# A ring of 21 weight tiles instead of 18, two of the tiles in a place of their own, and GpSimd's DMA scratch cut to 256 bytes

## The chip, the cores and the metric

The kernel runs on one core of one Trainium2 chip. The metric is the time of one execution on the device, in microseconds (us). Before the change the median of 3 runs is 1808.93 us, from 1807.16 to 1809.41.

The engines are named as the profile names them: PE is TensorE's matmuls, PEld its weight loads, DVE VectorE, ACT ScalarE, POOL GpSimd, SP SyncE, which only issues DMAs. A "q" behind a name (SPq) is that engine's sequencer, which issues DMAs and waits for semaphores.

## The reference

The program is a small transformer for 256 tokens of 1024 values in float32. The first block has two layers, each of a mixer (dilated attention in one half, gated linear attention in the other) and a dense SwiGLU network. The second block has one layer: modulation by a condition, a mixer of two kinds of attention, a router, and 32 experts, of which each token takes four.

```python
def second_block(x, c, w_ada, ...):
    mod = silu(c) @ w_ada + b_ada                  # 6 x 1024
    h = rms_norm(x, g_pre_mix) * (1 + sc_m) + sh_m
    proj = h @ w_in
    y_a = fox_attention(...)                       # forget gates: b_forget
    y_b = moba_attention(..., rel_bias)            # bias by distance
    x = x + gt_m * rms_norm(mix @ w_out, g_post_mix)
    h = rms_norm(x, g_pre_ffn) * (1 + sc_f) + sh_f
    x = x + gt_f * rms_norm(moe_ffn(h, ...), g_post_ffn)

def expert_block(xb, e):                           # rows of the tokens that chose e
    hdn = xb @ w_gate_up[e] + b_gate_up[e]         # 1024 -> 2048
    return clamped_swiglu(hdn) @ w_down[e] + b_down[e]   # 1024 -> 1024
```

The bias of the second attention depends on the distance of two tokens alone, so 384 values for each of 8 heads give the whole of it. The kernel writes them to DRAM once as a table (`toep`, each of the 8 rows repeated 128 times, 1536 KB), from which block 2 reads.

## The kernel before

**Weights.** All weights are read once, in tiles of 128 partitions x 2048 values, 1 MB each. SP issues the loads, in the order in which the program's scheduler puts them; a load whose place is still in use waits in SP's queue, and all loads behind it wait too. In block 1 the tiles go through the pool `ring` (4 places, `wtile()`); each is split into a high and a low part by ACT (the cast, L250) and DVE (the difference, L251), and PE multiplies three times (L256 to L258).

**Experts.** An expert is 12 tiles: 8 of `w_gate_up`, 4 of `w_down`. PE multiplies them unsplit: `g1` (L1209) takes the 8 gate_up tiles, 8 matmuls each, `act` makes the gated values `a` (tag "g"), and `g2` transposes them into `aT` (L1247) and multiplies the 4 down tiles (L1253). Experts with more than 64 tokens take a second pass under a branch (L1476, L1513). The tiles stand in the places of the ring RING2, in turn: -1 is one of the 4 places of `ring`, 0 to 7 are places of the pool `ring2`, which is opened when the second mixer's pool is closed, 8 to 12 of `ring3`, opened in the experts' phase, and HOME is the place of the hidden state, free once that is copied to DRAM (`homed`). The load of a tile waits until the matmuls of the tile 18 before it are through. The first EARLY = 10 tiles of expert 0 are asked for before the router (`first.load(EARLY)`), the rest when the pools are open.

**Block 1, first layer.** `early` work for block 2 is done there: GpSimd's queue loads `rel_bias` and `oh`, PE makes `rv` (8 x 384) from them, and GpSimd's queue stores `toep` (L821). `rv` has the tag "gkT", so that DVE's later copy gkT (L592) into the same place waits for the end of the store. The load of `bf` (L916), 8 values of the forget gate for block 2, has a place of its own that is free all along; the scheduler has it issued early, beside `gf` and `modb`, between two tiles of the first layer's `w_in`.

[...]

Of the kernel before, what the change touches and what calls it, by code (L numbers as in the profile page):

```python
# [9 lines left out]
F32 = mybir.dt.float32  # L10
# [10 lines left out]
P = 128  # L21
T = 256
D = 1024
KC = D // P
DFF = 2816
NF = DFF // P
NE = 32
# [5 lines left out]

HOME = 99
RING2 = (-1, 0, 1, -1, 2, 3, 4, 5, 6, 7, -1, -1, 8, 9, 10, 11, 12, HOME)
EARLY = 10

# [60 lines left out]
def kernel_body(ctx, tc, I, out, stop=None, dbg=None):  # L98
    nc = tc.nc
# [3 lines left out]
    xpool = ctx.enter_context(tc.tile_pool(name="xpool", bufs=1))  # L103
    spool = ctx.enter_context(tc.tile_pool(name="spool", bufs=4))
    ring = ctx.enter_context(tc.tile_pool(name="ring", bufs=4))
    dense = ctx.enter_context(ExitStack())
# [5 lines left out]
    def nm(s):  # L112
        uid[0] += 1
        return f"{s}_{uid[0]}"
# [4 lines left out]
    def wtile():  # L119
        return ring.tile([P, 2048], F32, tag="w", name=nm("w"))  # L120
# [666 lines left out]
    with ExitStack() as cx:  # L787
# [8 lines left out]
        starts = []  # L796
# [11 lines left out]
        def early():  # L808
            r = wtile()
            nc.scalar.dma_start(r[:, :9 * P], I["lev"])  # L810
            S.copy(wlev, r[:, :9 * P])
            rb = mix.tile([P, 8], F32, tag="kx", name="rb", bufs=2)
            G.memset(rb, 1.0)
            nc.gpsimd.dma_start(rb[0:NE, :], I["rel_bias"])
            oh = mix.tile([P, 384], F32, tag="X", name="oh")
            nc.gpsimd.dma_start(oh, I["oh"])
            q = ps()
            TE.matmul(q[0:8, :384], lhsT=rb, rhs=oh, start=True, stop=True)
            rv = mix.tile([8, 384], F32, tag="gkT", name="rv")
            V.tensor_copy(rv, q[0:8, :384])  # L820
            nc.gpsimd.dma_start(toep.rearrange("p a m -> a p m"), rv.unsqueeze(1).to_broadcast([8, P, 384]))  # L821
            S.activation(cond, cond, AF.Silu)
# [58 lines left out]
        def mixer2(x, start, late, done):  # L881
# [33 lines left out]
            bf = small(1, "bf", bufs=1)  # L915
            nc.sync.dma_start(bf[0:8], I["b_forget"].rearrange("o h -> h o"))  # L916
            S.activation(fT, f[0:8], AF.Identity, bias=bf[0:8, 0:1])
# [86 lines left out]
        g = {}  # L1004
# [134 lines left out]

        mixb = cx.enter_context(tc.tile_pool(name="mixb", bufs=1))  # L1140
        with tc.tile_pool(name="mix", bufs=1, side="right", reuse_waits="tile") as mix:
            rear = mixer2(x, starts[4], late_mix, done)
        ring2 = ctx.enter_context(tc.tile_pool(name="ring2", bufs=1, side="right", reuse_waits="tile"))
        turn = [0]

        def etile():
            i = RING2[turn[0] % len(RING2)]
            turn[0] += 1
            if i < 0:
                return wtile()  # L1150
            if i == HOME:
                return cpool.tile([P, 2048], F32, tag="h", name=nm("w2"))
            return (ring2 if i < 8 else ring3).tile([P, 2048], F32, tag=f"w{i}", name=nm("w2"))
# [24 lines left out]
        def expert(e):  # L1178
            return Expert(lambda kc: I["w_gate_up"][e, kc * P:(kc + 1) * P, :], lambda b: I["w_down_2"][e, b * 256:(b + 1) * 256, :], e == NE - 1)

        first = expert(0)
        first.load(EARLY)
        rear()
# [4 lines left out]
    with ExitStack() as cx:  # L1188
# [5 lines left out]
        bb = mo.tile([P, 2, 512], F32R, name="bb", bufs=1)  # L1194
        now = mo.tile([P, 9, NE], F32, name="now", bufs=1)
        qe = mo.tile([P, 2, NE], F32, name="qe", bufs=1)
# [43 lines left out]
        def g2(a, wd, y, j):  # L1240
# [3 lines left out]
            for i in range(4):  # L1244
                TE.transpose(q[:, i * P:(i + 1) * P], av[:, i // 2, i % 2, :], ident)
            aT = mo2.tile([P, 4, P], F32, tag="aT", name=nm("aT"), bufs=1)
            S.copy(aT.rearrange("p a b -> p (a b)"), q)  # L1247
# [60 lines left out]
        def extra_xt(slot0, pm):  # L1308
            op = mo.tile([P, 2, 32], F32R, tag="opos", name=nm("opos"), bufs=1)
            for t in range(2):  # L1310
                onehot(op[:, t, :], slot0, pm(t))
            xt = mo2.tile([P, KC, 32], F32, tag="aT", name=nm("oxt"), bufs=1)
            q = ps()
# [32 lines left out]
        def extra_out(a, slot0, pm, gt, wd, pg=None):  # L1346
# [7 lines left out]
            for j in range(2):  # L1354
                TE.transpose(q[:, j * P:(j + 1) * P], a.rearrange("p (n k) -> p k n", k=2)[:, j, :], ident)
            aT = mo2.tile([P, 4, P], F32, tag="aT", name=nm("oaT"), bufs=1)
            aT, oy = aT[:, :2, :], aT[:, 2:, :].rearrange("p a b -> p (a b)")
            S.copy(aT.rearrange("p a b -> p (a b)"), q[:, :256])
            oT = mo2.tile([P, T], F32, tag="oT", name=nm("oT"), bufs=1)
            turned(oT, pg)  # L1360
            q = ps()[:, :256]
# [31 lines left out]
        def many(spare):  # L1393

            most = nc.values_load(cmax[0:1, 0:1], min_val=0, max_val=2 * T)
            with tc.If(most > 96):  # L1396
                V.tensor_scalar_add(now[:, 0:2, :], posm, -96.0)
# [35 lines left out]
        psum = ctx.enter_context(tc.tile_pool(name="psum2", bufs=4, space=PSUM))  # L1433
        first.rest()
        nxt = begin(0, first)
        with tc.issue_after(order[TE].ins):
# [3 lines left out]
        for e in range(NE):  # L1440
# [23 lines left out]
            if e == 0:  # L1464
# [5 lines left out]
                G.memset(acc, 0.0)  # L1470
            more = mo2.tile([P, 256], F32, tag="og", name=nm("og"), bufs=1)
            pm, gt = (lambda t: posm[:, t, e:e + 1]), (lambda t: gate[:, t, e:e + 1])
# [110 lines left out]
```

## Time and profile before

| | |
|---|---|
| median of 3 runs | 1808.93 us |
| profiled execution | 1808.16 us |
| its span in the trace | 1806.4 us (1.76 us lie around it) |
| mean granted clock of PE | 0.984 |
| PE busy | 1700.8 us, 94% of the span |
| DVE, ACT, POOL busy | 792.5, 525.1, 146.6 us |
| DMA | 570.34 MB, mean 316 GB/s |
| loads of `w_gate_up` | 256 of 1 MB, 19.8 us from issue to landing |

PE is busy nearly all along, but a matmul that waits a short time for its tile shows as a longer distance to the next one rather than as much idle time, so waits are read from starts of matmuls. The experts' phase is the stretch from 827 us to the end, a little over half of the span, and it is there that the DMA row of the page is full.

### The profile page before, as it was taken

The numbers are of one execution on the slowest core, as the hardware profiler recorded it, in microseconds if no ns is written. First come the engines' busy times: TensorE is split into PE (matmuls) and PEld (weight loads), VectorE is DVE, ScalarE is ACT, GpSimd is POOL, SyncE is SP. The second block draws the span as 40 slices with busy tenths as digits, with TensorE's granted clock in tenths as the row PEclk, the third lists the DMA queues.
The fourth block names the chain that finished last, engine by engine and source line by source line (L and its number), as shares of the span: only waits on it lengthen the run. The fifth ranks groups of instructions, "written<-read, shape, count | busy, mean of one in ns | idle before, by whom it ended". The sixth has DMA issues, their size and how long they took to land. (4 is left out here: it accounts for less than half of the span.)

```text
span 1806.4 us, 23797 instructions
## 1 busy us (share of the span) xinstructions
PE 1700.8 (94%) x9464; PEld 1066.6 (59%) x9464; DVE 792.5 (44%) x1336; ACT 525.1 (29%) x898; POOL 146.6 (8%) x225
## 2 busy tenths in 40 slices
PE   7999999999999999989999999999989999899896
PEld 6887998788799978975533333334433333333232
DVE  5576677557767766763222212121321321212122
ACT  5645444465544445541101111010101110111011
POOL 1131220102211100100000000000000000000000
PEclk9999999999999999997999999999989999999999
DMA  9636688553478768478799999999989999999996
GB/s 318 148 129 201 222 276 279 186 167 105 167 232 266 267 228 264 145 292 333 294 371 419 418 419 418 418 418 418 417 363 418 418 419 418 419 418 418 419 418 264
DMA packets 160962, 570.34 MB, mean 316 GB/s; under 512 B 15490, under 2 KB 66188, under 8 KB 111636
## 3 DMA queue, kind: packets, MB, share of 16 engines
q1 hardware_dynamic: 149848, 553.47, 78.9%
q10 hardware_dynamic: 10140, 12.62, 2.2%
q0 software_dynamic: 800, 1.77, 0.9%
q8 instruction: 129, 2.11, 0.5%
q14 instruction: 45, 0.37, 0.1%
HBM read 564.11 MB, written 3.71 MB: 314 GB/s over the span
## 5 line engine op out<-in xcount | busy, mean ns | idle before, releaser
L1209 PE MATMUL g<-w,xt 128*64 128x512 f32 x2048 | 498.8, 601 | 25.0 <-PEq L1476 13.7
L1209 PEld LDWEIGHTS g<-w,xt 128*64 128x64 f32 x2048 | 152.5, 137 | 343.1 <-issue 319.1
L251 DVE TENSOR_TENSOR wlo<-w,whi 128x1024 fp32r<-128x1024 f32 x203 | 256.8, 1270 | 101.5 <-ACT whi L250 95.4
L250 ACT CAST whi<-w 128x1024 fp32r<-128x1024 f32 x203 | 211.3, 1046 | 186.6 <-PE ps L257 88.1
L1253 PE MATMUL ps<-w,aT 128*64 128x512 f32 x1024 | 230.5, 603 | 21.3 <-ACT aT L1247 21.3
L256 PE MATMUL ps<-xh,whi 128*128 128x256 f32 x792 | 226.0, 285 | 0.0
L257 PE MATMUL ps<-xh,wlo 128*128 128x256 f32 x792 | 223.6, 282 | 0.0
L258 PE MATMUL ps<-xl,whi 128*128 128x256 f32 x792 | 223.4, 282 | 0.0
L1231 DVE TENSOR_SCALAR g<-g 128x512 f32<-128x512 f32 x32 | 22.1, 692 | 414.8 <-PE g L1209 414.8
L1253 PEld LDWEIGHTS ps<-w,aT 128*64 128x64 f32 x1024 | 73.0, 138 | 158.3 <-issue 126.3
L1232 ACT ACTIVATE g<-g 128x512 f32<-128x512 f32 x32 | 19.3, 602 | 469.3 <-DVE g L1231 469.3
L256 PEld LDWEIGHTS ps<-xh,whi 128*128 128x128 f32 x792 | 149.9, 189 | 2.9 <-issue 2.3
L1256 DVE TENSOR_TENSOR yl<-ps,yh 64x512 fp32r<-64x512 f32 x64 | 44.1, 689 | 243.2 <-ACT yh L1255 242.2
L257 PEld LDWEIGHTS ps<-xh,wlo 128*128 128x128 f32 x792 | 150.0, 189 | 0.3
L258 PEld LDWEIGHTS ps<-xl,whi 128*128 128x128 f32 x792 | 149.9, 189 | 0.0
L1255 ACT CAST yh<-ps 64x512 fp32r<-64x512 f32 x64 | 37.1, 580 | 231.5 <-PE ps L1253 230.7
L1224 POOL CAST pick<-qe 128x128 fp32r<-128x128 f32 x32 | 9.5, 296 | 898.2 <-PE g L1226 889.0
L256 PE MATMUL ps<-whi,xh 128*128 128x512 f32 x176 | 72.0, 409 | 1.0 <-ACT xh L214 0.7
L257 PE MATMUL ps<-whi,xl 128*128 128x512 f32 x176 | 70.9, 403 | 1.2 <-DVE xl L215 1.2
L258 PE MATMUL ps<-wlo,xh 128*128 128x512 f32 x176 | 70.2, 399 | 0.0
L491 DVE SCALAR_TENSOR_TENSOR modm<-w,cond,modm 128x512 f32<-128x512 f32 x84 | 66.1, 787 | 8.7 <-DMA w<-in_w_ada_dram 7.0
L747 POOL TENSOR_TENSOR al<-sg,ah 128x256 fp32r<-128x256 f32 x36 | 44.6, 1239 | 209.3 <-ACT ah L746 209.3
(371 smaller groups left out, 2293.9 us busy)
## 6 DMA issues: line engine op xcount, KB each, us to landing
w<-in_w_gate_up_dram SPq DMA_DIRECT2D x256, 1024.0 KB, 19.8
w<-in_w_down_dram SPq DMA_DIRECT2D x149, 1024.0 KB, 19.8
w<-in_w_in_dram SPq DMA_DIRECT2D x32, 1024.0 KB, 7.2
w<-in_w_ada_dram SPq DMA_DIRECT2D x24, 1024.0 KB, 5.5
w<-in_w_gate_dram SPq DMA_DIRECT2D x22, 1024.0 KB, 7.8
w<-in_w_up_dram SPq DMA_DIRECT2D x22, 1024.0 KB, 5.1
w<-in_w_out_dram SPq DMA_DIRECT2D x12, 1024.0 KB, 4.9
w<-in_w_in_dram SPq DMA_DIRECT2D x8, 512.0 KB, 10.2
```

Of the source, the lines that this page charges most:

```text
L250: S.copy(hv, self.raw)
L251: V.tensor_sub(lv, self.raw, hv.bitcast(F32))
L256: TE.matmul(o, lhsT=ah, rhs=bh, start=first, stop=False)
L257: TE.matmul(o, lhsT=al, rhs=bh, start=False, stop=False)
L258: order[TE] = TE.matmul(o, lhsT=ah, rhs=bl, start=False, stop=last)
L491: V.scalar_tensor_tensor(m, w, c, m, ALU.mult, ALU.add)
L747: G.tensor_tensor(out=al[:, f, :], in0=a, in1=ah[:, f, :].bitcast(F32), op=ALU.subtract)
L1209: order[TE] = TE.matmul(banks[b][64 * a:64 * a + 64, :], lhsT=xt[:, kc, :], rhs=ws[kc][:, c0:c0 + 512], start=kc == 0, stop=kc == KC - 1)
L1231: V.tensor_scalar(out=a, in0=gl, scalar1=7.0, scalar2=None, op0=ALU.min)
L1253: TE.matmul(q[at[b], :], lhsT=aT[:, f % 4, 64 * (f // 4):64 * (f // 4) + 64], rhs=wd[f // 2][:, c0:c0 + 512], start=f == 0, stop=f == KC - 1)
L1255: S.copy(y[0][at[b], b, :], q[at[b], :])
L1256: V.tensor_tensor(out=y[1][at[b], b, :], in0=q[at[b], :], in1=y[0][at[b], b, :].bitcast(F32), op=ALU.subtract)
```

## The change

The ring gets 21 places. Two of them (`OWN`) are in a new pool `own` that nothing else uses, so they are free from the start; one more (13) is in `ring3`. `EARLY` becomes 12, of which the two own tiles are loaded directly behind the load of `bf` (`issue_after`), inside the second mixer's code, and the other ten where the ten were. `ex0` is made before the mixer for that.

Three more edits concern the on-chip memory. The scratch of GpSimd's DMAs is set to 256 bytes; with it the loads of `rel_bias` and `oh` and the store of `toep` go from GpSimd's queue to ACT's. In the experts' phase `now` takes the place of "og", `aT` and `oaT` the place of "g", and `oxt` the place of "oT"; in `extra_out` the turned places oT are made ahead of oaT.

```diff
--- before.py
+++ after.py
@@ -31,9 +31,10 @@
 
 AHEAD = 2
 
-HOME = 99
-RING2 = (-1, 0, 1, -1, 2, 3, 4, 5, 6, 7, -1, -1, 8, 9, 10, 11, 12, HOME)
-EARLY = 10
+
+HOME, OWN = 99, 100
+RING2 = (OWN, OWN + 1, -1, 0, 1, -1, 2, 3, 4, 5, 6, 7, -1, -1, 8, 9, 10, 11, 12, 13, HOME)
+EARLY = 12
 
 NREG = 4
 
@@ -102,6 +103,7 @@
     cpool = ctx.enter_context(tc.tile_pool(name="cpool", bufs=1))
     xpool = ctx.enter_context(tc.tile_pool(name="xpool", bufs=1))
     spool = ctx.enter_context(tc.tile_pool(name="spool", bufs=4))
+    own = ctx.enter_context(tc.tile_pool(name="own", bufs=1))
     ring = ctx.enter_context(tc.tile_pool(name="ring", bufs=4))
     dense = ctx.enter_context(ExitStack())
     psum = dense.enter_context(tc.tile_pool(name="psum", bufs=8, space=PSUM, reuse_waits="tile"))
@@ -811,14 +813,14 @@
             S.copy(wlev, r[:, :9 * P])
             rb = mix.tile([P, 8], F32, tag="kx", name="rb", bufs=2)
             G.memset(rb, 1.0)
-            nc.gpsimd.dma_start(rb[0:NE, :], I["rel_bias"])
+            nc.scalar.dma_start(rb[0:NE, :], I["rel_bias"])
             oh = mix.tile([P, 384], F32, tag="X", name="oh")
-            nc.gpsimd.dma_start(oh, I["oh"])
+            nc.scalar.dma_start(oh, I["oh"])
             q = ps()
             TE.matmul(q[0:8, :384], lhsT=rb, rhs=oh, start=True, stop=True)
             rv = mix.tile([8, 384], F32, tag="gkT", name="rv")
             V.tensor_copy(rv, q[0:8, :384])
-            nc.gpsimd.dma_start(toep.rearrange("p a m -> a p m"), rv.unsqueeze(1).to_broadcast([8, P, 384]))
+            nc.scalar.dma_start(toep.rearrange("p a m -> a p m"), rv.unsqueeze(1).to_broadcast([8, P, 384]))
             S.activation(cond, cond, AF.Silu)
 
         def finish(gpost, gpre, shift, nxt):
@@ -913,7 +915,8 @@
             f = ps()[:, :T]
             mm_feat(f, x, load_pad(w, 3072, 8))
             bf = small(1, "bf", bufs=1)
-            nc.sync.dma_start(bf[0:8], I["b_forget"].rearrange("o h -> h o"))
+            with tc.issue_after(nc.sync.dma_start(bf[0:8], I["b_forget"].rearrange("o h -> h o")).ins):
+                ex0.load(2)
             S.activation(fT, f[0:8], AF.Identity, bias=bf[0:8, 0:1])
             fb1 = out_([P, 8, T], "fb1")
             fb0 = out_([P, 8, P], "fb0")
@@ -1137,10 +1140,6 @@
                 V.tensor_copy(cnt[:, :NE], q[:, :NE])
                 V.tensor_reduce(out=cnt[:, NE:NE + 1], in_=q[:, :NE], axis=AX.X, op=ALU.max)
 
-        mixb = cx.enter_context(tc.tile_pool(name="mixb", bufs=1))
-        with tc.tile_pool(name="mix", bufs=1, side="right", reuse_waits="tile") as mix:
-            rear = mixer2(x, starts[4], late_mix, done)
-        ring2 = ctx.enter_context(tc.tile_pool(name="ring2", bufs=1, side="right", reuse_waits="tile"))
         turn = [0]
 
         def etile():
@@ -1148,6 +1147,8 @@
             turn[0] += 1
             if i < 0:
                 return wtile()
+            if i >= OWN:
+                return own.tile([P, 2048], F32, tag=f"own{i}", name=nm("w2"))
             if i == HOME:
                 return cpool.tile([P, 2048], F32, tag="h", name=nm("w2"))
             return (ring2 if i < 8 else ring3).tile([P, 2048], F32, tag=f"w{i}", name=nm("w2"))
@@ -1178,8 +1179,12 @@
         def expert(e):
             return Expert(lambda kc: I["w_gate_up"][e, kc * P:(kc + 1) * P, :], lambda b: I["w_down_2"][e, b * 256:(b + 1) * 256, :], e == NE - 1)
 
-        first = expert(0)
-        first.load(EARLY)
+        ex0 = expert(0)
+        mixb = cx.enter_context(tc.tile_pool(name="mixb", bufs=1))
+        with tc.tile_pool(name="mix", bufs=1, side="right", reuse_waits="tile") as mix:
+            rear = mixer2(x, starts[4], late_mix, done)
+        ring2 = ctx.enter_context(tc.tile_pool(name="ring2", bufs=1, side="right", reuse_waits="tile"))
+        ex0.load(EARLY - 2)
         rear()
         if stop == "mix2":
             return dump(h)
@@ -1192,7 +1197,6 @@
             nc.scalar.dma_start(homed[t], h[:, t, :])
 
         bb = mo.tile([P, 2, 512], F32R, name="bb", bufs=1)
-        now = mo.tile([P, 9, NE], F32, name="now", bufs=1)
         qe = mo.tile([P, 2, NE], F32, name="qe", bufs=1)
         xmh = mo.tile([P, 2, D], F32R, name="xmh", bufs=1)
         xml = xpool.tile([P, 2, D], F32R, tag="xl", name="xml")
@@ -1243,7 +1247,7 @@
             av = a.rearrange("p (b n k) -> p b k n", b=2, k=2)
             for i in range(4):
                 TE.transpose(q[:, i * P:(i + 1) * P], av[:, i // 2, i % 2, :], ident)
-            aT = mo2.tile([P, 4, P], F32, tag="aT", name=nm("aT"), bufs=1)
+            aT = mo2.tile([P, 4, P], F32, tag="g", name=nm("aT"), bufs=1)
             S.copy(aT.rearrange("p a b -> p (a b)"), q)
             qs = [ps(), ps()]
             at = [slice(64 * (b ^ j), 64 * (b ^ j) + 64) for b in range(2)]
@@ -1309,7 +1313,7 @@
             op = mo.tile([P, 2, 32], F32R, tag="opos", name=nm("opos"), bufs=1)
             for t in range(2):
                 onehot(op[:, t, :], slot0, pm(t))
-            xt = mo2.tile([P, KC, 32], F32, tag="aT", name=nm("oxt"), bufs=1)
+            xt = mo2.tile([P, KC, 32], F32, tag="oT", name=nm("oxt"), bufs=1)
             q = ps()
             for kc in range(KC):
                 for t in range(2):
@@ -1353,11 +1357,11 @@
             q = ps()
             for j in range(2):
                 TE.transpose(q[:, j * P:(j + 1) * P], a.rearrange("p (n k) -> p k n", k=2)[:, j, :], ident)
-            aT = mo2.tile([P, 4, P], F32, tag="aT", name=nm("oaT"), bufs=1)
+            oT = mo2.tile([P, T], F32, tag="oT", name=nm("oT"), bufs=1)
+            turned(oT, pg)
+            aT = mo2.tile([P, 4, P], F32, tag="g", name=nm("oaT"), bufs=1)
             aT, oy = aT[:, :2, :], aT[:, 2:, :].rearrange("p a b -> p (a b)")
             S.copy(aT.rearrange("p a b -> p (a b)"), q[:, :256])
-            oT = mo2.tile([P, T], F32, tag="oT", name=nm("oT"), bufs=1)
-            turned(oT, pg)
             q = ps()[:, :256]
             for f in range(KC):
                 for i in range(4):
@@ -1393,6 +1397,7 @@
         def many(spare):
 
             most = nc.values_load(cmax[0:1, 0:1], min_val=0, max_val=2 * T)
+            now = mo2.tile([P, 9 * NE], F32, tag="og", name="now", bufs=1).rearrange("p (a e) -> p a e", a=9)
             with tc.If(most > 96):
                 V.tensor_scalar_add(now[:, 0:2, :], posm, -96.0)
                 V.tensor_copy(now[:, 2:4, :], gate)
@@ -1431,8 +1436,8 @@
         xt = pick_up(g["xt"])
         dense.close()
         psum = ctx.enter_context(tc.tile_pool(name="psum2", bufs=4, space=PSUM))
-        first.rest()
-        nxt = begin(0, first)
+        ex0.rest()
+        nxt = begin(0, ex0)
         with tc.issue_after(order[TE].ins):
             ahead = places(), slot_gates(0)
             ns = counts(0)
@@ -1468,7 +1473,7 @@
                         V.tensor_sub(xml[:, t, :], xm[:, t, :], xmh[:, t, :].bitcast(F32))
                 acc = xpool.tile([P, 2, D], F32, tag="xh", name="acc")
                 G.memset(acc, 0.0)
-            more = mo2.tile([P, 256], F32, tag="og", name=nm("og"), bufs=1)
+            more = mo2.tile([P, 9 * NE], F32, tag="og", name=nm("og"), bufs=1)[:, :256]
             pm, gt = (lambda t: posm[:, t, e:e + 1]), (lambda t: gate[:, t, e:e + 1])
             sel = lambda q: qe[:, q, e:e + 1]
 
@@ -1568,7 +1573,7 @@
     import concourse.bacc as _bacc
     from concourse.bass_utils import run_bass_kernel_spmd as _run
 
-    nc = _bacc.Bacc("TRN2", target_bir_lowering=False, num_devices=1)
+    nc = _bacc.Bacc("TRN2", target_bir_lowering=False, num_devices=1, dynamic_dma_scratch_size=256)
     arrays, aps = {}, {}
     for name, a in layout(inputs).items():
         a = np.ascontiguousarray(a)

```

Three places show how the order of instructions moves. The first is SP's queue in block 1's first layer, before the change; `w_748` and `w_750` are tiles of `w_in`:

```order
16 L272 DMA w_648<-in_w_in_dram 128x8x256
17 L265 DMA w_748<-in_w_in_dram 128x4x512
18 L484 DMA modb_1801<-in_b_ada_dram 24x128
19 L1015 DMA gf<-in_g_post_ffn_dram 128x8
20 L916 DMA bf_6854<-in_b_forget_dram 8x1
21 L265 DMA w_750<-in_w_in_dram 128x4x512
22 L265 DMA w_924<-in_w_in_dram 128x4x512
23 L265 DMA w_926<-in_w_in_dram 128x4x512
```

And after it, where `w_751`, `w_753` and `w_927` are the same tiles as `w_748`, `w_750` and `w_924`:

```order
16 L274 DMA w_651<-in_w_in_dram 128x8x256
17 L267 DMA w_751<-in_w_in_dram 128x4x512
18 L486 DMA modb_1804<-in_b_ada_dram 24x128
19 L1018 DMA gf<-in_g_post_ffn_dram 128x8
20 L918 DMA bf_6857<-in_b_forget_dram 8x1
21 L1165 DMA w_1266_6859<-in_w_gate_up_dram 128x2048
22 L1165 DMA w_1267_6861<-in_w_gate_up_dram 128x2048
23 L267 DMA w_753<-in_w_in_dram 128x4x512
24 L267 DMA w_927<-in_w_in_dram 128x4x512
25 L267 DMA w_929<-in_w_in_dram 128x4x512
```

The two loads of `w_gate_up` behind `bf` are the own tiles of expert 0. They now stand in SP's queue in block 1, ahead of the tile w_753.

The second is ACT in the same stretch, before; `whi_493` is the cast of a padded tile of `w_in` (16 columns), `whi_535` and `whi_586` those of the next tile:

```order
31 L608 DMA A_739<-in_msk_dram 128x576
32 L531 COPY s_346<-ps_277 128x512
33 L564 DMA sr_521<-in_gla_w_gate_up_dram 16x256
34 L565 DMA sr_521<-in_gla_b_gate_dram 1x256
35 L250 CAST whi_493<-w_490 128x1024
36 L450 ACTIVATE qT_172<-ps_393 128x4x128
37 L448 COPY kbd_173<-ps_399 128x4x128
38 L250 CAST whi_535<-w_532 128x1024
39 L250 CAST whi_586<-w_532 128x1024
40 L414 ACT_TABLE_LOAD
41 L414 ACTIVATE s_421<-s_421,nmx_432 128x128 x4
42 L555 COPY v_63_368<-ps_371 128x8x64
```

And after, with the names `whi_496`, `whi_538` and `whi_589` for these three:

```order
33 L610 DMA A_742<-in_msk_dram 128x576
34 L533 COPY s_349<-ps_280 128x512
35 L566 DMA sr_524<-in_gla_w_gate_up_dram 16x256
36 L823 DMA toep<-rv 8x128x384
37 L452 ACTIVATE qT_175<-ps_396 128x4x128
38 L450 COPY kbd_176<-ps_402 128x4x128
39 L416 ACT_TABLE_LOAD
40 L416 ACTIVATE s_424<-s_424,nmx_435 128x128 x4
41 L416 ACTIVATE s_457<-s_457,nmx_468 128x128 x4
42 L557 COPY v_63_371<-ps_374 128x8x64
43 L557 COPY v_63_371<-ps_375 128x8x64
44 L252 CAST whi_496<-w_493 128x1024
```

The store of toep has come in ahead of qT, and the cast of the padded tile, which stood ahead of qT, now stands behind both groups of exps and both copies of v; the two casts of the next tile, which stood ahead of the table load, follow it (rows 46 and 47 of that listing).

The third is SP where the ring comes to its end for the first time, before; `ball` is the experts' bias:

```order
166 L1164 DMA w_1497_8111<-in_w_gate_up_dram 128x2048
167 L1164 DMA w_1498_8113<-in_w_gate_up_dram 128x2048
168 L1164 DMA w_1499_8115<-in_w_gate_up_dram 128x2048
169 L1218 DMA ball<-in_b_gate_up_dram 64x2x512 x2
170 L1164 DMA w_8150<-in_w_gate_up_dram 128x2048
171 L1164 DMA w_1502_8152<-in_w_gate_up_dram 128x2048
```

And after:

```order
168 L1165 DMA w_1499_8117<-in_w_gate_up_dram 128x2048
169 L1165 DMA w_1500_8119<-in_w_gate_up_dram 128x2048
170 L1165 DMA w_1501_8121<-in_w_gate_up_dram 128x2048
171 L1173 DMA w_1502_8123<-in_w_down_dram 128x2048
172 L1222 DMA ball<-in_b_gate_up_dram 64x2x512 x2
173 L1173 DMA w_1504_8158<-in_w_down_dram 128x2048
174 L1173 DMA w_1505_8160<-in_w_down_dram 128x2048
```

The bias load now follows 21 tiles in place of 18, two of which were asked for in block 1.

## Rows read from the trace of the kernel before

**Rows 1.** Section 2 of the page: GB/s in 40 slices of the span, 45.2 us each.
```profile
GB/s 318 148 129 201 222 276 279 186 167 105 167 232 266 267 228 264 145 292 333 294 371 419 418 419 418 418 418 418 417 363 418 418 419 418 419 418 418 419 418 264
```

**Rows 2.** Timeline of PE, expert 30: start, us, engine, line, operation, tiles, count, [idle before].
```profile
1739.33 8.80 PE L1209 MATMUL g<-w,xt 128*64 128x512 f32 x40
...
1750.16 0.50 PE L1290 MATMUL ps<-yh,pT 128*128 128x512 f32 x1
```

**Rows 3.** Windows of 12 us: busy times, PEclk, DMA share, GB/s (the last three columns).
```profile
892.00:904.00 12.00, 10.79 (x103) 5.32 (x100) 2.95 (x8) 2.28 (x5) 0.00 (x0) 1.00 0.31 119
...
928.00:940.00 12.00, 11.85 (x53) 4.14 (x51) 1.38 (x2) 1.16 (x2) 0.30 (x1) 1.00 0.66 264
...
952.00:964.00 12.00, 11.85 (x50) 3.80 (x50) 1.92 (x5) 1.18 (x3) 0.00 (x0) 1.00 1.02 423
```

**Rows 4.** Timeline of SP's DMA queue where the ring is first full.
```profile
830.78 2.74 SPq L1164 DMA_DIRECT2D w<-in_w_gate_up_dram  x2
```

**Rows 5.** Timeline of PE, experts 27, 28 and 31.
```profile
1644.89 5.67 PE L1209 MATMUL g<-w,xt 128*64 128x512 f32 x24
1651.12 1.94 PE L1209 MATMUL g<-w,xt 128*64 128x512 f32 x8 [0.56 <-DMA w<-in_w_gate_up_dram]
...
1657.97 0.36 PE L1377 MATMUL ps<-pos,xmh 128*128 128x192 f32 x1
...
1675.97 7.09 PE L1209 MATMUL g<-w,xt 128*64 128x512 f32 x32
1683.53 1.94 PE L1209 MATMUL g<-w,xt 128*64 128x512 f32 x8 [0.48 <-DMA w<-in_w_gate_up_dram]
...
1766.65 1.94 PE L1209 MATMUL g<-w,xt 128*64 128x512 f32 x8
...
1780.69 1.13 PE L1306 MATMUL fin<-acc,idio 128*128 128x512 f32 x2
```

**Rows 6.** The same timeline, the stop in expert 28.
```profile
1690.41 1.98 PE L1209 MATMUL g<-w,xt 128*64 128x512 f32 x4 [4.94 <-PEq L1476]
```

**Rows 7.** Waits of PEld, 827 to 1806: waited for, us in total, times, longest.
```profile
PEld g L1209 <- DMA w<-in_w_gate_up_dram: 21.5, 23, 1.4
```

**Rows 8.** Timelines of ACT, its queue and SP's queue in block 1.
```profile
39.36 0.52 ACTq L565 DMA_DIRECT2D sr<-in_gla_b_gate_dram  x1
42.10 1.05 ACT L250 CAST whi<-w 128x1024 fp32r<-128x1024 f32 x1 [2.68 <-DMA gf<-in_g_post_ffn_dram]
...
54.59 0.57 ACT L555 COPY v<-ps 128x512 f32<-128x512 f32 x1
```
```profile
38.44 0.33 SPq L916 DMA_DIRECT2D bf<-in_b_forget_dram  x1
44.49 14.87 SPq L265 DMA_DIRECT2D w<-in_w_in_dram  x3
```

**Rows 9.** Timeline of PE in block 1.
```profile
53.04 0.28 PE L256 MATMUL ps<-xh,whi 128*128 128x256 f32 x1
...
70.38 1.57 PE L430 MATMUL ps<-v,pT 128*128 128x65 f32 x8 [1.93 <-ACT pT L423]
```

**Rows 10.** What the trace has of toep, and who waits at its end.
```profile
L821 POOL DMA_DIRECT2D toep<-rv x1: 1172/1172/1172, 40.2 to 40.2; - x1
...
DMA to landing us min/median/max: 35.6/35.6/35.6
```
```profile
75.93 0.42 DVE L592 COPY gkT<-ps 128x256 f32<-128x256 f32 x1 [4.36 <-DMA toep<-rv]
```
```profile
76.84 1.05 ACT L250 CAST whi<-w 128x1024 fp32r<-128x1024 f32 x1 [6.51 <-DMA w<-in_w_in_dram]
```

**Rows 11.** Windows of 5 us in block 1, columns as in rows 3.
```profile
65.00:70.00 5.00, 3.44 (x28) 2.91 (x24) 3.86 (x7) 3.25 (x5) 0.00 (x0) 1.00 0.51 68
...
75.00:80.00 5.00, 5.00 (x28) 4.74 (x28) 2.67 (x7) 3.13 (x4) 0.00 (x0) 0.73 0.81 303
```

**Rows 12.** Timeline of PE, the down matmuls of expert 31.
```profile
1785.60 0.65 PE L1253 MATMUL ps<-w,aT 128*64 128x512 f32 x2 [0.74 <-ACT aT L1247]
```

## The prediction

> **What bounds the kernel now.** I read the row of GB/s over the span first, then TensorE's waits for tiles in the experts' phase, then the stretches in which the ring was full, and last the stretch of block 1 to which the diff moves DMAs. The row of GB/s [rows 1] stands at 417 to 419 from its 22nd slice on, with one dip. One tile is 1 MB (1.049 million bytes), so the stream needs 1.049 / 0.4185 = 2.51 us for it and 12 x 2.51 = 30.1 us for an expert. TensorE is quicker: in expert 30 the six tiles from 1739.33 to 1750.16, which wait for nothing, take 10.83 us, or 1.80 each [rows 2]. So the stream is the slower of the two, and TensorE lives on the lead that the ring of 18 slots has stored. The ring was full early in the phase: at 892 to 904 the core moved 119 GB/s, at 928 to 940 264, and from 952 to 964 423 without a break [rows 3]; in the full stretches SP issues each load in the instant that TensorE lets a tile go [rows 4]. From there the lead shrinks until the tiles come late, in experts 27, 28 and 31 [rows 5]. The stall of 4.94 us at 1690.41 is not one of these: its row names TensorE's own sequencer at the branch L1476 [rows 6], and the change leaves it.
>
> **Term 1, the late tiles.** Six tiles without a wait are 10.83 us [rows 2]. In expert 27 the six from 1644.89 to 1657.97 take 13.08: 2.25 lost. In expert 31 the six from 1766.65 to 1780.69 take 14.04: 3.21 lost. In expert 28 the four from 1675.97 to 1683.53 take 7.56 against 4/5 x 8.80 = 7.04 from the 40 matmuls of expert 30: 0.5 lost. Together 5.95 us [rows 2, 5]. (The profile sums 21.5 us of weight loads that waited for a gate_up tile, in 23 waits [rows 7]; a weight load runs ahead of its matmul, so the smaller number counts.) Three more slots put the stream three tiles ahead wherever the ring is full: 3 x 2.51 = 7.5 us. The full stretches remain, so the lead is really filled: at 892 to 904 alone the DMA gave up (418 - 119)/418 x 12 = 8.6 us [rows 3]. 7.5 is more than 5.95, so the waits go as a whole, and what is late next is TensorE itself with 1.5 us to spare. Ends of this term: -5.0 (a lead of two tiles only, 2 x 2.51, so that 0.95 us of waiting stays) and -7.5 (the whole lead, if more of the 21.5 us counts than I can see on TensorE). I take -5.95, which is nearest to the matmuls' own rows.
>
> **Term 2, ACT's order in block 1.** The toep store, and the loads of oh and rel_bias, go from GpSimd's queue to ACT's, and with them the cast of the padded weight tile (L250, 42.10 in the trace) moves behind the two groups of exps and the two copies of v, of which the last ends at 55.16 [rows 8]. The cast (1.05) then ends near 56.2 and the difference on VectorE, about as long again, near 57.4; TensorE wants them for the narrow matmuls at 53.04 [rows 9]. It waits 3.2 to 4.4 us there. Cover: its idle 1.93 us before 70.38 [rows 9], and then the wait of ACT until 76.84 and of VectorE until 75.93, which both stand ahead of the next exps and have another cause [rows 10]. [...] I cost it at +0.5, with 0 and +2.5 (4.4 less 1.93) as ends. That the issue of three DMAs on ACT takes some 0.5 us each [rows 8] is inside these ends. What is freed on GpSimd (1.17 us [rows 10]) is worth nothing, its share of the span being small.
>
> **Term 3, the two own tiles.** They hang on the load of bf, and SP has that load early in block 1: so 2 MB enter the queue at about 39 to 43 us, in front of the w_in tile that SP issues at 44.49 [rows 8]. That tile is the one that ACT waits 6.51 us for, to 76.84 [rows 10]: 32 us for 1 MB. The reason is toep: issued at 40.20, landed 35.6 us later, at 75.8. From 65 to 70 the DMA engines are busy to 0.51, about eight of sixteen, and move 68 GB/s, of which toep is 1.57 MB / 35.6 us = 44; from 75 to 80, with toep gone, it is 303 [rows 11]. So the half of the tile that falls to toep's eight engines waits for toep's end. Of the own tiles 1 MB falls to these engines as well, ahead of the tile. If none of it is through before toep takes hold, the tile comes 1.049 / 0.303 = 3.5 us later, and so does TensorE, since cast, exps and transposes follow one another. If the own tiles are through by then (the queue was not full at 40) it costs nothing, and toep then holds the same bytes as before. Further ends: -1.9 (the tile is early, and TensorE's 1.93 us of idle goes) and +5.0 (both own tiles whole, 2 x 2.51, on the path). Two of them leave at 39 to 43, before toep's bulk, so I take +1.0, nearer to the free end.
> The trace gives toep 44 GB/s for eight partitions [rows 10]. [...]
>
> **The rest.** Buffers shared in the experts' phase (aT with g, now with og, the turned places before oaT) cost nothing by TensorE's order: g's readers are through when aT is written, and aT's readers, the down matmuls, stand ahead of the next expert's gate_up matmuls, which VectorE must await before it writes g. The cover is that order; a wait of 0.1 us in each of 32 experts would be 3.2. In the experts' first loads SP issues expert 0's last two tiles earlier, and the bias load behind three more tiles; the ring is full by 830.78 [rows 4], so what is needed there has long been asked for. Nothing.
>
> **Sum.** -5.95 + 0.5 + 1.0 = -4.45 us. The profiled execution took 1808.16 (span 1806.4 and 1.76 around it), so 1803.7 on it; it lies 0.8 below the median 1808.93, so 1804.5 against that. I forecast 1804.2. What a measurement of this kernel can tell from no change is about 0.2%, 3.6 us.
>
> **Rivals.**
> A. The own tiles sit in front of the w_in tile: term 3 is +3.5 and term 2 +1.5. Then -5.95 + 5 = -1: 1807.9, no change that can be told. For it: 6.51 us of waiting at just this tile. Against: both leave before toep's bulk.
> B. Slower: toep, from ACT's queue, is itself held up by the own tiles (2 MB / 418 GB/s = 5 us on its engines), lands at 81, and only then pass the remaining halves of the own tiles and of the w_in tile, 1.57 million bytes, in 1.57 / 0.303 = 5.2 us: the tile lands at 86 instead of 76.8, +9.4. With the 2.5 of term 2 not hidden, +11.9 - 5.95 = +6: 1814.5. It decides once block 1 is longer by 9.6 us (5.95 + 3.6). For it: toep's engines are full already. Against: after toep's end the DMA engines pass 303 GB/s, so eight of them could pass far more than toep's 44, and part of its time is a wait that other packets can use.
> C. The change doesn't do what it says: the lead is filled by two tiles only or lost in a full ring, or TensorE meets the next limit at once; the expert phase gives 3 us, block 1 takes 1.5: 1807. For it: the stall at 1690.41 shows that TensorE has other stops. Against: after 1344 the stream is unbroken [rows 1].
> D. Faster still: toep goes quicker on the other queue, or spreads over sixteen engines, and the waits to 75.93 and 76.84 go with the 1.93 of idle and the slow clock's 1.35: -5.95 - 3.3 = -9.25: 1799.3. For it: the waits of ACT and VectorE on toep. Against: TensorE itself was busy for most of them. [...]
>
> **Chances.** Forecast 0.46, D 0.14, A 0.17, C 0.10, B 0.13. The forecast's own range is 1802 to 1806.5, and 4.45 is little over 3.6, so a quarter of it (0.12) falls within 0.2%. Faster: 0.34 + 0.14 = 0.48; within 0.2%: 0.12 + 0.17 + 0.10 = 0.39; slower: B's 0.13. The range takes in A, C and D, and of B only the foot: 1799 to 1811.5.
>
> **What would show it.** Right: no wait of TensorE for a gate_up tile in experts 27, 28 and 31, six tiles in 10.83 us in each; the own tiles' two loads at 39 to 43; the down matmuls of the last expert about 4.5 us earlier than at 1785.60 [rows 12]. Terms 2 and 3 show in block 1: a wait of TensorE of 3 to 4 us at 53, and the w_in cast at 76 to 81. It is wrong if that cast comes after 82, if TensorE still waits for tiles past 1640, or if block 1 as a whole ends more than 3 us later than before.

## The result and the profile after

The changed kernel takes 1827.23 us (median of 5 runs, 1823.78 to 1827.73); the kernel before, timed beside it, 1808.93 (1806.32 to 1815.54). The ratio is 1.0090, with a 95% interval from 1.0076 to 1.0103: slower by 14 to 19 us, where I had forecast 4 to 5 us less. The medians are 18.3 us apart, and the profiled execution has a span of 1824.4 us, 18.0 above that of before.

The time is lost in two steps, and the gain of the ring does not come at all. TensorE reaches expert 0 at 843.55 instead of 827.07, which is 16.5 late, and of that 16.0 arise in block 1 before 100 us. Experts 0 to 4 add 4.4: they take 163.5 us at a granted clock of 0.94, against 159.0 at 0.97. TensorE is 21.9 late at expert 13 and 18.0 at the end.

Block 1 first. The timelines of ACT and of its queue in the changed kernel:

```profile
38.92 0.33 ACTq L566 DMA_DIRECT2D sr<-in_gla_w_gate_up_dram  x1
39.88 0.54 ACTq L823 DMA_DIRECT2D toep<-rv  x1
...
53.21 0.23 ACTq L567 DMA_DIRECT2D sr<-in_gla_b_gate_dram  x1
53.65 0.58 ACT L557 COPY v<-ps 128x512 f32<-128x512 f32 x1
54.13 1.05 ACT L252 CAST whi<-w 128x1024 fp32r<-128x1024 f32 x1
```

And every wait of TensorE in the same stretch, 50 to 80:

```profile
55.23 0.39 PE L258 MATMUL ps<-xh,whi 128*128 128x256 f32 x1 [2.06 <-ACT whi L252]
56.54 0.58 PE L259 MATMUL ps<-xh,wlo 128*128 128x256 f32 x1 [0.93 <-DVE wlo L253]
75.92 2.04 PE L575 MATMUL ps<-sr 128*128 128x256 f32 x4 [11.65 <-issue]
```

The cast is late as forecast, and costs 3 us of waiting at 55 [rows 8, 9]. The large loss is the third row: the gate matmuls read `sr`, into which 1 KB of `gla_b_gate` is loaded. Before, toep went through GpSimd's queue, and this load through ACT's with no store ahead of it [rows 8, 10]; now it stands behind toep in ACT's own queue. The third row names no releaser ("issue"), but the trace has the packets that the DMA engines moved: toep's 1024 run from 43.72 to 75.46, and the one packet of the gate load, on the same queue, at 75.32, 22.1 us after its issue. The matmuls start at 75.92.

The experts' phase: the row of GB/s of the page, and the tiles of experts 27 and 31 in the timeline of PE.

```profile
GB/s 341 144 103 163 227 263 273 230 163 116 119 251 264 276 272 209 174 239 389 307 294 420 417 419 418 418 419 417 420 306 419 418 418 419 418 418 419 418 417 270
```
```profile
1663.61 5.37 PE L1213 MATMUL g<-w,xt 128*64 128x512 f32 x24
1669.49 1.94 PE L1213 MATMUL g<-w,xt 128*64 128x512 f32 x8 [0.51 <-DMA w<-in_w_gate_up_dram]
...
1676.34 0.36 PE L1381 MATMUL ps<-pos,xmh 128*128 128x192 f32 x1
...
1784.63 1.94 PE L1213 MATMUL g<-w,xt 128*64 128x512 f32 x8
...
1798.91 1.56 PE L1310 MATMUL fin<-acc,idio 128*128 128x512 f32 x3
```

The six tiles of expert 27 take 12.73 us and those of expert 31 14.28, against 13.08 and 14.04 before [rows 5]: the tiles are as late as they were. The dip of the 30th slice has become deeper, 306 for 363 [rows 1]. What stands in it is a row of SP's waits over the experts' phase, which I had not read. Before, and after:

```profile
SPq L1164 <- DMA yl<-in_b_down_dram: 17.4, 1, 17.4
```
```profile
SPq L1165 <- DMA yl<-in_b_down_dram: 23.5, 1, 23.5
```

In expert 16, ACT loads the experts' second bias, `b_down`, into a buffer that is free only then. One load of SP's waits for that load to land, and all tiles behind it wait too. The trace shows what ties them: the two report their landing on the same semaphore, and SP issues the tile less than 0.1 us after b_down has landed (at 1341.04 for 1341.02 before, at 1359.53 for 1359.47 after). That holds in all five kernels in which SP stops here (before, after, and experiments 1, 3 and 8); in experiments 2 and 4 b_down has a semaphore to itself, and SP doesn't wait for it. SP issues its last load at 1323.29 (before) and 1335.62 (after) and the next at 1341.04 and 1359.53, each time the sixth tile of expert 17. Each of these rows joins the two loads around the stop, before and after:

```profile
1323.29 18.07 SPq L1164 DMA_DIRECT2D w<-in_w_gate_up_dram  x2
```
```profile
1335.62 24.24 SPq L1165 DMA_DIRECT2D w<-in_w_gate_up_dram  x2
```

From there to the end of the span it is 465.4 us before and 464.8 after. So the end of the kernel is the instant at which `b_down` lands plus the stream of the tiles that are left, and this instant hangs on how late TensorE and ACT reach expert 16. The larger ring let SP come to its stop earlier, 21.8 us ahead of b_down's issue for 13.3, and wait longer there, 23.5 us for 17.4.

### The profile page after: what moved, and what is told of

Same layout as the page of the kernel before. It is cut to its first block, busy times and chain, and to the rows that moved or that the text cites. A ratio compares the mean times of both kernels' runs of the same rounds, so it can differ in the third digit from the quotient of the medians.

```text
span 1824.4 us, 23796 instructions
## 1 busy us (share of the span) xinstructions
PE 1706.7 (94%) x9464; PEld 1072.0 (59%) x9464; DVE 793.2 (43%) x1336; ACT 525.9 (29%) x898; POOL 143.2 (8%) x222
## 5 line engine op out<-in xcount | busy, mean ns | idle before, releaser
L1213 PE MATMUL g<-w,xt 128*64 128x512 f32 x2048 | 501.6, 603 | 25.0 <-PEq L1481 14.3
L1235 DVE TENSOR_SCALAR g<-g 128x512 f32<-128x512 f32 x32 | 22.1, 692 | 417.3 <-PE g L1213 417.3
```

The costliest lines, as they stand in the source:

```text
L1213: order[TE] = TE.matmul(banks[b][64 * a:64 * a + 64, :], lhsT=xt[:, kc, :], rhs=ws[kc][:, c0:c0 + 512], start=kc == 0, stop=kc == KC - 1)
L1235: V.tensor_scalar(out=a, in0=gl, scalar1=7.0, scalar2=None, op0=ALU.min)
```

## The experiments

Each is timed beside the kernel before, whose median was then 1810.05 us (experiments 1 to 4), 1810.38 (5 to 7) and 1808.97 (8 and 9). The starts of the first gate_up matmuls of experts 0 and 17, and the end, are from each kernel's profiled execution; that of experiment 2 is the fastest of its four, 4.9 us below their median, the others lie within 2.3 of theirs. "Late at 100" says how much later the matmuls around 100 us start than in the kernel before. Two kernels with the same code up to there can differ in it: the changed kernel is 16.0 late, experiment 2 14.7.

| kernel | expert 0 | expert 17 | end | 17 to end | median | ratio to before (95%) |
|---|---|---|---|---|---|---|
| before | 827.1 | 1355.7 | 1806.4 | 450.7 | 1808.9 | |
| after | 843.6 | 1374.5 | 1824.4 | 449.9 | 1827.2 | 1.0090 (1.0076 to 1.0103) |
| 1 gate load on SP | 831.1 | 1358.7 | 1810.0 | 451.3 | 1812.7 | 1.0015 (1.0003 to 1.0026) |
| 2 b_down on GpSimd | 838.4 | 1372.7 | 1812.6 | 439.9 | 1819.3 | 1.0055 (1.0038 to 1.0073) |
| 3 before, toep on ACT | 844.2 | 1373.2 | 1823.6 | 450.4 | 1824.3 | 1.0073 (1.0055 to 1.0091) |
| 4 before, b_down on GpSimd | 827.8 | 1358.2 | 1804.8 | 446.6 | 1808.9 | 0.9995 (0.9982 to 1.0008) |
| 5 gate on SP, b_down early, ring 20 | 831.0 | 1358.1 | 1802.4 | 444.3 | 1803.8 | 0.9962 (0.9946 to 0.9977) |
| 6 toep behind gate and cast, ring 20 | 832.9 | 1361.4 | 1804.5 | 443.1 | 1805.1 | 0.9968 (0.9957 to 0.9979) |
| 7 the same, ring 18 | 830.7 | 1357.1 | 1807.1 | 450.0 | 1811.0 | 1.0004 (0.9995 to 1.0013) |
| 8 after, own tiles in block 2 | 845.0 | 1376.1 | 1825.9 | 449.8 | 1826.1 | 1.0091 (1.0073 to 1.0108) |
| 9 as 6, own tiles in block 2 | 828.9 | 1357.3 | 1801.1 | 443.8 | 1802.6 | 0.9964 (0.9950 to 0.9978) |

**1. The gate load on SP's queue.**

```diff
-        nc.scalar.dma_start(wg[32:33, :], I["gla_b_gate"][lay:lay + 1, :])
+        nc.sync.dma_start(wg[32:33, :], I["gla_b_gate"][lay:lay + 1, :])
```

> The changed kernel with one edit: the 1 KB load of gla_b_gate goes to SP's queue, where it stands before the own tiles, instead of ACT's, where it stands behind the toep store. Theory (the gate matmuls L575 wait 11.65 us at 75.92 because that load is served behind toep's 1.5 MB in ACT's queue): that wait is gone, the gate matmuls run at about 64, and with the lower clock around the gap 11 to 13 us of the 16 us of block 1 go: about 1815. The 4.9 us at 53 to 57 (cast order) stay. Rival (the own tiles in front of the w_in tile, or the w_in loads themselves, hold block 1): the gate matmuls are early but TensorE stops again a few matmuls later for the w_in tile that SP issues at 56.5 and for the next one at 75.9, and less than 4 us go: about 1824.

1812.7 us, 14.5 below the changed kernel. The matmuls of the gate in its timeline of PE, and the first of the waits at 55, which stays:

```profile
55.03 0.39 PE L258 MATMUL ps<-xh,whi 128*128 128x256 f32 x1 [2.06 <-ACT whi L252]
...
63.66 1.03 PE L575 MATMUL ps<-sr 128*128 128x256 f32 x4
```

The theory holds and the rival falls: 1 KB in the wrong place of a queue was 14 of the 16 us. At 100 us TensorE is 1.7 late, although it was 4.7 late at 57: the waits of ACT (6.51) and VectorE (4.36) [rows 10] are gone from this trace, and with them 3 us of the late cast are absorbed.

**2. b_down through GpSimd's queue.**

```diff
-                        nc.scalar.dma_start(bd, I["b_down"])
+                        nc.gpsimd.dma_start(bd, I["b_down"])
```

> The changed kernel with one edit: the load of b_down in expert 16 goes to GpSimd's queue instead of ACT's. Theory (the lead of the larger ring is lost at expert 16, where SP's queue waits 23.5 us for that load): SP no longer waits for it, the stream loses its dip at slice 29, the lead of 7.5 us reaches expert 31, and TensorE waits for no tile past 1640: 5.5 to 7 us less, about 1820.5. Rival (the ring is full there and would stop SP anyway, or TensorE itself is the next limit): the dip stays and the tiles of experts 27 and 31 are late as before, within 2 us of 1827.

1819.3 us, 8 below the changed kernel. SP's wait for b_down is gone. The bottom of the dip in the changed kernel, the stretch here in which b_down is loaded (GB/s is the last column), and TensorE's wait for b_down itself, which grew from 1.54 us in the changed kernel to 5.67:

```profile
1354.00:1360.00 6.00, 4.27 (x23) 2.29 (x20) 5.02 (x8) 0.97 (x2) 0.53 (x2) 1.00 0.09 23
```
```profile
1348.00:1360.00 12.00, 5.68 (x28) 2.92 (x25) 5.95 (x11) 0.97 (x2) 1.27 (x3) 0.77 1.01 415
```
```profile
1357.85 1.24 PE L1344 MATMUL ps<-yl,gT 32*128 32x256 f32 x8 [5.67 <-DMA yl<-in_b_down_dram]
```

From expert 17 to the end it is 439.9 us instead of 449.9: the lead of the ring arrives once SP is not stopped for b_down. SP still stops, from 1356.28 to 1375.58, but there it waits for TensorE to let a place go: the ring is full. Past 1640 TensorE waits 1.4 us for tiles, against 4.8 in the changed kernel; the theory had none.

**3. The kernel before with toep on ACT's queue.**

```diff
-            nc.gpsimd.dma_start(toep.rearrange("p a m -> a p m"), rv.unsqueeze(1).to_broadcast([8, P, 384]))
+            nc.scalar.dma_start(toep.rearrange("p a m -> a p m"), rv.unsqueeze(1).to_broadcast([8, P, 384]))
```

> The kernel before with one edit: the toep store goes to ACT's queue. No own tiles, ring of 18. Theory (ACT's queue is the cause in block 1, the gate load behind toep and the cast behind the exps): TensorE waits 2 to 4 us at 53 and then for the gate load until about 76, block 1 ends 15 to 17 us later, about 1825. Rival (the two own tiles in SP's queue are the larger part): 3 to 6 us later, about 1813.

1824.3 us. One edit of the change, without ring and own tiles, makes most of its loss (1.0073 of 1.0090). Here the wait names its cause:

```profile
74.23 2.04 PE L573 MATMUL ps<-sr 128*128 128x256 f32 x4 [9.51 <-DMA sr<-in_gla_b_gate_dram]
```

At 100 us it is 14.2 late, against 16.0 and 14.7 in the two kernels with the whole change in block 1, so the own tiles account for 0.5 to 1.8, hardly more than these two differ by.

**4. The kernel before with b_down through GpSimd's queue.** The edit of experiment 2.

> The kernel before with one edit: the load of b_down in expert 16 goes to GpSimd's queue. Ring of 18. Theory (SP's wait of 17.4 us for that load, and not the size of the ring, costs the lead that is missing in experts 27 to 31): the stream runs on through 1332 to 1344, gains the 6 us that it gave up there, and the late tiles of 27 and 31 go but for a rest: 4 to 6.5 us less, about 1803.5. Rival (18 places are full there, so SP stops for TensorE a moment later): less than 1 us, about 1808.

0.9995, no difference that can be told, so the rival is the nearer one. SP's waits around expert 16 are now others:

```profile
SPq L1164 <- PEq L1513: 15.4, 2, 12.8
...
SPq L1164 <- PEq L1476: 11.0, 2, 6.1
```

With 18 places SP runs into the places that TensorE has not yet let go; both names are branches of TensorE's program. From expert 17 to the end 4 us are gained (446.6 for 450.7), but TensorE reaches expert 17 2.5 us later, with 5.5 us of waiting for b_down in place of 3.85.

**5. Both, with b_down in a place of its own.** b_down is loaded on ACT's queue when the experts' phase begins; its 1 KB in each partition costs the ring one place.

```diff
-RING2 = (OWN, OWN + 1, ..., 12, 13, HOME)
+RING2 = (OWN, OWN + 1, ..., 12, HOME)
+        bd = mo.tile([P, 256], F32, name="bd", bufs=1)
+        nc.scalar.dma_start(bd, I["b_down"])
...
-                        nc.scalar.dma_start(bd, I["b_down"])
```

> The changed kernel with two edits together: gla_b_gate on SP's queue as in the first experiment, and b_down loaded on ACT's queue at the start of the experts' phase into 1 KB of its own, for which the ring gives up one place (20). Theory (the two waits are separate and each holds its own part): block 1 as in the first experiment, SP never waits for b_down, TensorE does not wait for it in expert 16, and a lead of 5.0 us (two places more than 18) reaches the end: 1812.7 - 2 (wait of TensorE in expert 16) - 5 (late tiles) = about 1806, from 1803 to 1808. Rival (the lead is lost elsewhere too, for example at the branches where SP's queue waits for TensorE's sequencer): the tiles of experts 27 and 31 are late as before, and it stays at 1810 to 1813.

1803.8 us, faster than the kernel before: 0.9962. TensorE has no wait for b_down, and late tiles are left in expert 31 alone (the row of PE's waits from 1600 on):

```profile
PE g L1215 <- DMA w<-in_w_gate_up_dram: 1.7, 3, 0.6
```

**6. toep behind the gate load and the cast.** gla_b_gate is back on ACT's queue, the rest is as in 5; `store` issues toep, which the code of block 1 no longer does, and `cast` is the cast of the padded tile, which is now asked for ahead of its matmuls.

```diff
+        b_gate = nc.scalar.dma_start(wg[32:33, :], I["gla_b_gate"][lay:lay + 1, :])
+        if lay == 0:
+            with tc.issue_after(b_gate.ins), tc.issue_after(cast):
+                store()
```

> As the run before it, but block 1 put in order in another way: gla_b_gate stays on ACT's queue, and the toep store is issued behind that load and behind the cast of the padded tile. Theory (the cast that came late at 53 costs the 1.7 us that are left of block 1): TensorE's stop at 53 is gone or under 1 us, block 1 ends within 1 us of the kernel before, and the whole is 1 to 2 us below the run before it, about 1804: faster than both kernels. Rival (what is left in block 1 comes from the own tiles ahead of the w_in tile): block 1 ends 1.5 us late all the same, about 1806.

1805.1 us, no better than 5. The stop at 53 is gone, as the theory has it, but one of 1.41 and 0.44 us has come at 58, for the cast of the next tile, and block 1 is 5.5 us late at 100, where the theory had less than 1 and the rival 1.5. VectorE's wait for toep's end, and when ACT issued toep:

```profile
82.54 0.42 DVE L600 COPY gkT<-ps 128x256 f32<-128x256 f32 x1 [7.78 <-DMA toep<-rv]
```
```profile
46.70 0.29 ACTq L830 DMA_DIRECT2D toep<-rv  x1
```

**7. The same with 18 places and no own tiles.**

> As the run before it, with the ring of 18 and without own tiles: the first ten tiles of expert 0 before the router, as in the kernel before. So only the queues and the early b_down differ from the kernel before. Theory (the two own places are worth their 5.0 us of lead once SP does not wait for b_down): the tiles of experts 27 to 31 come late by what the lead lacks; SP runs on in expert 16 until 18 places are full, which the fourth experiment showed to be worth about half of the 6 us: 1.5 to 4 us above the run before it, about 1807. Rival (without SP's wait for b_down 18 places are enough): within 1 us of it.

1811.0 us, 1.0004: 6.0 above experiment 6, where the theory had 1.5 to 4. Between 6 and 7 stand only the two own places with their early loads: from expert 17 to the end they are worth 6.9 us (450.0 less 443.1), and by experiments 5 and 9, with the same ring, 5.7 and 6.2. The rival falls. With 18 places the early b_down alone gains nothing there (450.0 for 450.7): SP issues the third tile of expert 18 at 1359.93, where it did so at 1358.60 before, each time after a wait for TensorE to let a place go. So the stop and the size of the ring have to go together. This kernel also has the small scratch and the shared buffers, and they cost nothing that can be told. Block 1 is 0.1 late at 100; toep left at 43.79 and VectorE waited less:

```profile
78.65 0.42 DVE L600 COPY gkT<-ps 128x256 f32<-128x256 f32 x1 [4.17 <-DMA toep<-rv]
```

So the order on ACT's queue is the cause in block 1, apart from what the own tiles add.

**8. The changed kernel with the own tiles in block 2.**

```diff
-            with tc.issue_after(nc.sync.dma_start(bf[0:8], ...).ins):
+            nc.sync.dma_start(bf[0:8], ...)
+            with tc.issue_after(order["sp"].ins):      # the last w_in tile asked for so far
                 ex0.load(2)
```

> The changed kernel with one edit: the two own tiles are asked for in block 2, behind four tiles of its w_in, instead of in block 1 behind bf. Theory (the own tiles in block 1 are a small part of its 16 us; the gate load behind toep is the rest): block 1 ends 1 to 3 us earlier, as the third experiment without own tiles did (14.2 us late against 16.0), the experts' phase is the same: about 1825. Rival (the 2 MB in front of toep and the w_in tile hold block 1): 8 us or more go.

1826.1 us, 13.9 late at 100, against 16.0 and 14.7 with the own tiles in block 1: they cost 0.8 to 2.1 us there, and the theory's 1 to 3 is the nearer one. The packets agree: from its issue to its last packet toep takes 35.0 to 36.0 us in the five kernels with the own tiles in block 1 and toep on ACT's queue, and 34.0 to 34.5 in the four without them. SP stops for b_down as in the changed kernel, and from its restart at 1360.93 to the end it is 465.0:

```profile
SPq L1166 <- DMA yl<-in_b_down_dram: 23.4, 1, 23.4
```

**9. Experiment 6 with the own tiles in block 2.** The edit of experiment 8.

> The sixth experiment (toep issued behind the gate load and the cast, b_down early, ring of 20) with the own tiles asked for in block 2, behind four tiles of its w_in. Theory (in the sixth experiment toep was issued at 46.7 instead of 43.8 in the seventh, behind the landing of an own tile, and its end held the copy gkT until 82.5 instead of 78.7; without own tiles in block 1 that is gone): block 1 ends as in the seventh, 0.1 us above the kernel before instead of 5.5, and the rest as in the sixth: 1805.0 - 5.4 = about 1799.6. Rival (in block 2 the 5 us of loads in front of w_in tiles cost as much): about 1804.

1802.6 us, 0.9964: with experiment 5 the fastest, and faster than both kernels, but 3 us above what I expected. The store of toep is issued at 43.79, as in 7, and block 1 is 1.9 late at 100, for 5.5 in experiment 6 and 0.1 in 7. From expert 17 to the end it is 443.8 us, for 443.1 in experiment 6: the waits for late tiles are 4.8 us in place of 1.7, and a stop of 2.2 us at the branch in expert 28 is 0.2 here (PE's waits from 1640 on):

```profile
PE g L1222 <- DMA w<-in_w_gate_up_dram: 4.8, 9, 0.6
```

## Why the prediction was wrong

- **Term 1 (-5.95).** The amount was read rightly and the premise wrongly. The step that failed is "From there the lead shrinks": I took the lead of 892 to 964 to be handed on to expert 31. It is thrown away at expert 16, where SP waits for b_down; I had passed over the place as "one dip". 465.4, 464.8, 464.9 (experiment 1, restart at 1345.20), 465.4 (experiment 3, 1358.22) and 465.0 us from SP's restart to the end, with rings of 18 and 21 alike, show that nothing ahead of the restart but its time matters. With the stop removed the places pay as the term said, or a little more: 5.7 to 6.9 us for two (7 against 5, 6 and 9), and 6.7 for three (4 against 2).
- **Term 2 (+0.5).** The late cast was found in the order and sized well: 2.06 + 0.93 us of waiting; in experiment 1, where it stands alone, 4.7 of delay at 57 with the slower clock around it (its 128x256 matmuls stand 0.21 us apart from 56.9 to 59.5 and 0.12 from 59.9 on; in the changed kernel the granted clock was 0.83 from 50 to 60), and 1.7 left at 100. What failed is its inventory. In the order of ACT shown ahead of the prediction the gate load is row 34 (L565) before the change; after it, toep is row 36, and the gate load isn't among the rows up to 44, so it comes later still. I priced the instruction that moved behind the exps and not the DMA that moved behind 1.5 MB. That was 14.3 us (16.0 less 1.7 of experiment 1).
- **Term 3 (+1.0).** 0.5 to 2.1 us (16.0 and 14.7 less 14.2 and 13.9), inside its ends and around the value taken. In the order of experiment 6 the own tiles cost more, 3.6 us (5.5 less 1.9 of experiment 9). The tile of w_in did not become the bound. The halves that the term speaks of are in the traces: of the 16 landings of the w_in tile issued at 44.49 in the kernel before, eight come by 49.18 and eight from 75.94 to 76.76; of those of the second own tile, issued at 43.14 in the changed one, eight by 48.15 and eight from 60.07 to 61.81.
- **Toep on the other queue.** It took 35.6 us from its issue to its last packet on ACT's queue (39.88 to 75.46), and 35.6 to its landing on GpSimd's [rows 10]: rival D falls. What the move cost its new neighbours, 14.3 us, was in none of my terms.
- **Rivals.** B had the right sign, about a third of the size (1814.5 at its point, 1827.2 measured) and another mechanism; the changed kernel does not show its w_in tile holding TensorE. A's 3.5 us for the own tiles were not reached in the changed kernel. C's "lost in a full ring" came nearest for the experts. In D the slow clock's 1.35 us is 5 x 0.27, from the 0.73 of [rows 11]; the change did not win it: from 0 to 100 us the mean granted clock was 0.97 before and 0.90 in the changed kernel.
- **"The rest" (nothing).** From expert 5 to expert 13 it is 228.2 us before (986.1 to 1214.3) and 229.2 after (1007.0 to 1236.2), so the shared buffers cost at most 1 us.
- **The signs of being wrong** came, all three. The cast that stands at 76.84 before is at 89.06, though no longer with a wait for its tile: the work ahead of it is late; past 1640 TensorE waits 4.8 us for tiles; block 1 ends 16.0 late.
- Open: the 4.94 us at the branch in expert 28 [rows 6]. The longest wait at that branch past 1640 is 4.8 after, 3.0 and 2.2 in experiments 5 and 6, and 0.2 in 2, 8 and 9. In 8 the late tiles take its place (10.1 us of waits for 4.8) and the end does not move. What makes it I have not shown, nor why the clock of experts 0 to 4 was lower in the changed kernel.

## What to carry to other kernels

When a DMA is moved to another engine's queue, list what stands behind it there, down to the smallest load, and ask who waits for each: here a load of 1 KB behind a store of 1.5 MB came 22.1 us after its issue, and TensorE stood idle 11.65 us for it. Before paying for a deeper prefetch ring, look in the loading queue's own waits for a load that waits for something other than a free place, such as a DMA of another engine that reports on the same semaphore: here the lead was set back at such a point, and the deeper ring only waited there longer (23.5 us for 17.4). Here the stop had to go and the ring had to grow; either alone gained nothing that can be told. A dip in a flat row of GB/s is a place to read the waits of, not a detail.

## What the runs showed of the hardware

- A load of 1 KB, issued on ACT's queue at 53.21 behind a store that still ran, let its reader start at 75.92, 22.7 us later; on SP's queue, ahead of 2 MB of tiles, the same load was in time (the reader at 63.66 waited for nothing).
- On one queue that load's packet waited for the store's: 75.32 in the changed kernel, 73.63 in experiment 3, each just ahead of the store's last packets (75.46 and 74.23).
- The store of 1.5 MB from 8 partitions took 34.0 to 36.0 us on ACT's queue and 35.6 on GpSimd's.
- The load of b_down (128 KB) landed 2.1 us after its issue in the changed kernel, where SP had issued nothing for 21.8 us, and 4.4 in the kernel before, where it was 13.3. Through GpSimd's queue, beside an unbroken stream of 414 to 415 GB/s, it took 6.0 and 5.8 (experiments 2 and 4), and TensorE waited 5.67 and 5.5 us for it instead of 1.54 and 3.85. That the queue makes the difference is not shown: through ACT's queue, issued at 822 beside 424 GB/s (822 to 830 in experiment 5), it took 7.1 and 6.7 (experiments 5 and 7).
